# Output projection of a hybrid decoder layer: one weight pool to the end, the group's first sums made a group ahead, norm weights multiplied on GpSimd

## The chip, the cores and the metric

The kernel runs on one core of a Trainium2 chip. The metric is the time of one execution on the device in microseconds (us); lower is better. Before the change three executions took 2694.65, 2693.23 and 2694.86 us, median 2694.65. The engines are named as in the profile: PE (TensorE, with its weight loads PEld), DVE (VectorE), ACT (ScalarE), POOL (GpSimd) and SP (SyncE, which here only issues transfers).

## The reference, cut to what matters

One layer on 256 tokens of width 4096, in float32. The input is normalised and projected by `w_in` (4096 x 21024); two token mixers (a sliding-window attention and a gated delta rule) run on the projections and are merged by gates. What this change touches is the end:

```
merged = sigmoid(gate_a) * y_a + sigmoid(gate_b) * y_b
out = einsum('btd,de->bte', merged, w_o)        # 256 x 4096 by 4096 x 4096
x = x + rms_norm(out, post_norm_g)              # out * rsqrt(mean(out^2) + eps) * post_norm_g
```

## The kernel before, in words

**Precision.** PE multiplies numbers of a rounded 32-bit type. To keep float32 accuracy each weight tile `raw` is split in two: `hi` is the rounded copy, made by ACT (line 174), and `lo` is what the rounding left, made by DVE as `raw - hi` (line 175). A product (`product`, lines 865 to 868) is three matmuls into the same PSUM bank: activations hi by weights hi, hi by lo, lo by hi. `split` works on 1024 columns of a tile at a time, so each call is one ACT cast and one DVE subtraction of 128x1024.

**Order.** The kernel is written in program order and a planner in the framework orders the instructions of each engine when the kernel is compiled: it lets time pass by its own estimates and gives an engine, whenever that is free, the ready instruction that comes first by priority and then by program order. `urgent(2)` marks the splits and the sums of weights as the most pressing, `urgent(1)` the copies out of PSUM; matmuls, transfers and the work of `beside` have none. A tile comes from a pool with a fixed number of buffers, and its first writer waits until the last reader of the buffer's old content is done. On the chip each engine then runs its list strictly in order.

**The stages at the end.** After the merge, `chunk(0)` (line 880) makes the first 512 of the 4096 output columns: 8 loads of 1 MB (`load`, line 190), each split in two units, each unit 12 matmuls. Then pools are closed (lines 994 to 996): `mpool` (the merged activations), `evpool`, and the pool `weights` with 3 buffers each of `raw` (1 MB), `hi` and `lo` (512 KB). A new pool `weights2` takes their place, with 3 buffers of `raw` and 4 each of `hi` and `lo` (`wide`), and the pool `outp` for the output.

Then come three blocks (`block`, line 899), each 1024 output columns in 8 groups of 512 rows of `w_o`. A block computes its 2 x 2 product (two halves of 128 tokens, two halves of 512 columns) with seven products instead of eight for part of the rows, so some products use sums of weight tiles. Per group there are two loads of 1 MB, `rs` (line 913) and `rp` (line 914), and six units, each split and then multiplied: two sums of rs (`tt`, line 918, and line 919, which writes over the second tile of rs) and unit one, rs[0:2]; unit two, rp[0:2]; unit three, rs[2:4]; unit four, rp[2:4]; unit five, the sums tt[0:2]; unit six, the sum tt[2]. Lines 929 and 934 make the other sums. A group is 15 products, 45 matmuls of 512 columns, into eight PSUM banks.

When a block ends, ACT copies its eight banks to SBUF (line 955), and the rest is done while the next block runs: `sums` and `more` on DVE (lines 957 to 966), `norm` on ACT (squares, line 970), and `scale` (lines 972 to 976): for each half a load of the norm's weights `pg` (one buffer, `pg_load`) and one DVE multiplication of 128x1024. The work beside the third block's results falls into `chunk(7)`, which makes the last 512 columns; there the four loads of `x` (`xr`, line 1023) also run. `finish` (line 1028) scales and adds, and stores the output.

Of the kernel before, what the change touches and what calls it, by code (L numbers as in the profile page):

```python
# [8 lines left out]
F32 = mybir.dt.float32  # L9
F32R = mybir.dt.float32r  # L10
# [43 lines left out]
def tile_hybrid_mixer(  # L54
# [18 lines left out]
    V, S, G, PE = nc.vector, nc.scalar, nc.gpsimd, nc.tensor  # L73

    cp = ctx.enter_context(tc.tile_pool(name="consts", bufs=1, side="left"))
    wpool_ = tc.tile_pool(name="weights", bufs=3, side="left")
    wp = wpool_.__enter__()
    evpool = tc.tile_pool(name="evac", bufs=4, side="left")
    ev = evpool.__enter__()
    mp = ctx.enter_context(tc.tile_pool(name="psmain", bufs=5, space=PSUM))  # L80
# [78 lines left out]
        return tc.high_priority(offset=1000000 * level)  # L159

    newest = {}
    wide = {}
    unit = [0]


    def split(raw, extra=False):
        if extra:
            both = wp.tile([P, 4, 512], F32R, name="both", tag="raw")
            hi, lo = both[:, 0:2], both[:, 2:4]
        else:  # L170
            hi = wp.tile([P, 2, 512], F32R, name="hi", **wide)
            lo = wp.tile([P, 2, 512], F32R, name="lo", **wide)
        with urgent(2):
            newest["hi"] = S.copy(hi, raw).ins  # L174
            newest["lo"] = V.tensor_tensor(lo, raw, hi.bitcast(F32), op=ALU.subtract).ins  # L175
        return hi, lo
# [722 lines left out]
    def block(b, beside):  # L899
# [5 lines left out]
        def raws(k2):  # L905
            raw = wp.tile([P, 4, 512], F32, name="raw")
            src = w_o[k2 * 256:k2 * 256 + 256, n0:n0 + 1024].rearrange("(k p) n -> p k n", p=P)
            nc.sync.dma_start(raw.rearrange("p (k h) n -> p k (h n)", k=2), src)
            return raw

        for c in range(8):
            f, l = c == 0, c == 7
            rs = raws(2 * c)
            rp = raws(2 * c + 1)
            kt = 4 * c
            tt = op_.tile([P, 3, 512], F32, name="tt")
            with urgent(2):
                V.tensor_tensor(tt[:, 0], rs[:, 1], rs[:, 3], op=ALU.add)
                V.tensor_tensor(rs[:, 1], rs[:, 0], rs[:, 1], op=ALU.add)
            hi, lo = split(rs[:, 0:2])  # L920
            product(m1, *plain(kt, 0), hi[:, 0], lo[:, 0], f, l)
            product(m5, *form(c, 1), hi[:, 1], lo[:, 1], f, l)
            hi, lo = split(rp[:, 0:2])
            product(m2, *plain(kt + 2, 0), hi[:, 0], lo[:, 0], f, False)
            product(m3, *plain(kt + 2, 0), hi[:, 1], lo[:, 1], f, False)
            product(n4, *plain(kt + 2, 1), hi[:, 0], lo[:, 0], f, False)
            product(x8, *plain(kt + 2, 1), hi[:, 1], lo[:, 1], f, False)
            with urgent(2):
                V.tensor_tensor(tt[:, 1], rs[:, 1], rs[:, 3], op=ALU.add)
            hi, lo = split(rs[:, 2:4])  # L930
            product(m2, *plain(kt + 1, 0), hi[:, 0], lo[:, 0], False, False)
            product(m3, *form(c, 0), hi[:, 1], lo[:, 1], False, False)
            with urgent(2):
                V.tensor_tensor(tt[:, 2], tt[:, 1], rs[:, 2], op=ALU.add)
            hi, lo = split(rp[:, 2:4])
            product(m2, *plain(kt + 3, 0), hi[:, 0], lo[:, 0], False, l)
            product(m3, *plain(kt + 3, 0), hi[:, 1], lo[:, 1], False, l)
            product(x8, *plain(kt + 3, 1), hi[:, 1], lo[:, 1], False, l)
            product(n4, *plain(kt + 3, 1), hi[:, 0], lo[:, 0], False, False)
            hi, lo = split(tt[:, 0:2])  # L940
            product(m7, *form(c, 3), hi[:, 0], lo[:, 0], f, l)
            product(m6, *form(c, 2), hi[:, 1], lo[:, 1], f, l)
            hi = wp.tile([P, 2, 512], F32R, name="hi", **wide)
            lo = wp.tile([P, 2, 512], F32R, name="lo", **wide)
            with urgent(2):
                S.copy(hi[:, 0], tt[:, 2])
                V.tensor_tensor(lo[:, 0], tt[:, 2], hi[:, 0].bitcast(F32), op=ALU.subtract)
            product(n4, *plain(kt + 1, 1), hi[:, 0], lo[:, 0], False, l)
            if c in beside:
                beside[c]()  # L950
        st = op_.tile([P, 4, 512], F32, name="st")
        w1, w2 = slice(n0, n0 + 512), slice(n0 + 512, n0 + 1024)
        with urgent(1):
            for d_, bank in ((st[:, 0], m1), (st[:, 1], m5), (u[:, 0, w1], m2), (u[:, 0, w2], m3), (u[:, 1, w2], x8), (st[:, 3], m7), (st[:, 2], m6), (u[:, 1, w1], n4)):
                S.copy(d_, bank)

        def sums():
# [14 lines left out]
        def scale():  # L972
            for h in range(2):
                pg = pg_load(1 + 2 * b + h)
                cs = slice(n0 + 512 * h, n0 + 512 * h + 512)
                V.tensor_tensor(u[:, :, cs], u[:, :, cs], mid(pg, 2), op=ALU.mult)

        return {0: sums, 1: more, 2: norm, 4: scale}

# [13 lines left out]
    ps, _ = chunk(0, forms)  # L993
    mpool.__exit__(None, None, None)
    evpool.__exit__(None, None, None)
    wpool_.__exit__(None, None, None)
    wp = ctx.enter_context(tc.tile_pool(name="weights2", bufs=3, side="left"))
    wide = {"bufs": 4}
    op_ = ctx.enter_context(tc.tile_pool(name="outp", bufs=1, side="left"))
    u = op_.tile([P, 2, D], F32, name="u")  # L1000
    so = R[:, 0:18].rearrange("p (a b) -> p a b", a=2)
# [87 lines left out]
```

## Time and profile before

| | us |
|---|---|
| median of three executions | 2694.65 |
| the profiled execution | 2694.28 |
| its span in the profile | 2692.6 |
| PE busy in the span | 2666.9 |
| DVE busy | 1769.8 |
| ACT busy | 1330.6 |
| POOL busy | 38.5 |

The span runs from the first to the last instruction that the profile shows; the execution's own time is 1.68 us more. Busy time is summed over the span, and a matmul counts as busy until its modelled end, so matmuls overlap and small gaps of PE don't show in it; the distance from one matmul's start to the next tells more. Line numbers are those of the kernel before.

### The profile page before, as it was taken

The numbers are of one execution on the slowest core, as the hardware profiler recorded it, in microseconds if no ns is written. First come the engines' busy times: TensorE is split into PE (matmuls) and PEld (weight loads), VectorE is DVE, ScalarE is ACT, GpSimd is POOL, SyncE is SP. The second block draws the span as 40 slices with busy tenths as digits, with TensorE's granted clock in tenths as the row PEclk, the third lists the DMA queues.
The fourth block names the chain that finished last, engine by engine and source line by source line (L and its number), as shares of the span: only waits on it lengthen the run. The fifth ranks groups of instructions, "written<-read, shape, count | busy, mean of one in ns | idle before, by whom it ended". The sixth has DMA issues, their size and how long they took to land.

```text
span 2692.6 us, 37957 instructions
## 1 busy us (share of the span) xinstructions
PE 2666.9 (99%) x15164; PEld 2311.8 (86%) x15164; DVE 1769.8 (66%) x2463; ACT 1330.6 (49%) x1926; POOL 38.5 (1%) x59
## 2 busy tenths in 40 slices
PE   9999999999999999999999999999999999989998
PEld 7888888888888888888888888888888888867876
DVE  8785876776776454555554665665555555869996
ACT  7445445545445444444444544555444444546554
POOL 0100100000000000000000000000000000000000
PEclk9999999999999999999999999999999999999999
DMA  8554555655555555565665455455566655645556
GB/s 276 166 178 156 185 173 164 191 165 168 185 174 168 192 188 188 188 189 190 193 193 193 150 180 171 157 180 166 190 192 192 190 188 188 191 175 191 207 213 242
DMA packets 249425, 499.90 MB, mean 186 GB/s; under 512 B 22048, under 2 KB 22688, under 8 KB 248736
## 3 DMA queue, kind: packets, MB, share of 16 engines
q1 hardware_dynamic: 247952, 495.36, 56.6%
q8 instruction: 119, 1.95, 0.3%
q10 hardware_dynamic: 1296, 2.11, 0.2%
q14 instruction: 58, 0.48, 0.0%
HBM read 491.93 MB, written 5.24 MB: 185 GB/s over the span
## 4 chain that ended last, share of the span: by engine, by line
PE 90%; DVE 6%; issue 1%; DMA 1%; ACT 1%; SPq 0%; POOL 0%; DVEq 0%; POOLq 0%; ACTq 0%
PE mm L232 48%; PE mm L233 25%; DVE lo L175 3%; PE mm L867 3%; PE mm L868 3%; PE mm L866 2%; PE mm L226 2%; PE sd L868 1%; PE sd L867 1%; PE sd L866 1%; PE mm L225 1%; DVE pr L508 1%; DVE xs L509 1%; DMA xt<-in_xT_dram 1%; PE sd L769 1%
## 5 line engine op out<-in xcount | busy, mean ns | idle before, releaser
L232 PE MATMUL mm<-hT,hi 128*128 128x512 f32 x5083 | 1788.4, 393 | 0.2 <-ACT hi L185 0.2
L175 DVE TENSOR_TENSOR lo<-raw,hi 128x1024 fp32r<-128x1024 f32 x909 | 1106.1, 1223 | 745.2 <-ACT hi L174 743.4
L174 ACT CAST hi<-raw 128x1024 fp32r<-128x1024 f32 x909 | 948.4, 1049 | 1183.8 <-PE mm L232 1042.9
L233 PE MATMUL mm<-hT,lo 128*128 128x256 f32 x5083 | 1435.2, 282 | 2.2 <-DVE lo L175 1.4
L232 PEld LDWEIGHTS mm<-hT,hi 128*128 128x128 f32 x5083 | 954.2, 188 | 199.8 <-issue 7.9
L233 PEld LDWEIGHTS mm<-hT,lo 128*128 128x128 f32 x5083 | 960.3, 189 | 16.6 <-DVE lo L175 8.4
L232 PE MATMUL mm<-gbs,hi 128*128 128x512 f32 x480 | 168.0, 390 | 0.0
L232 PE MATMUL mm<-gas,hi 128*128 128x512 f32 x480 | 168.0, 390 | 0.0
L233 PE MATMUL mm<-gbs,lo 128*128 128x256 f32 x480 | 135.3, 282 | 0.0
L233 PE MATMUL mm<-gas,lo 128*128 128x256 f32 x480 | 135.3, 282 | 0.0
L866 PE MATMUL mm<-hi,ms 128*128 128x512 f32 x268 | 106.6, 400 | 8.2 <-ACT hi L174 8.2
L867 PE MATMUL mm<-lo,ms 128*128 128x512 f32 x268 | 107.0, 399 | 0.3 <-DVE lo L175 0.3
L868 PE MATMUL mm<-hi,ms 128*128 128x512 f32 x268 | 106.5, 397 | 0.0
L232 PEld LDWEIGHTS mm<-gas,hi 128*128 128x128 f32 x480 | 90.1, 188 | 17.8
L232 PEld LDWEIGHTS mm<-gbs,hi 128*128 128x128 f32 x480 | 90.1, 188 | 17.8
L241 ACT COPY cr<-mm 128x256 f32<-128x256 f32 x228 | 83.8, 367 | 20.1 <-PE mm L226 18.1
L233 PEld LDWEIGHTS mm<-gbs,lo 128*128 128x128 f32 x480 | 90.7, 189 | 1.3
L233 PEld LDWEIGHTS mm<-gas,lo 128*128 128x128 f32 x480 | 90.6, 189 | 1.3
L866 PEld LDWEIGHTS mm<-hi,ms 128*128 128x128 f32 x268 | 50.4, 189 | 22.5 <-ACT hi L174 10.7
L226 PE MATMUL mm<-hT,hi 128*128 128x512 f32 x164 | 64.3, 392 | 0.0
L867 PEld LDWEIGHTS mm<-lo,ms 128*128 128x128 f32 x268 | 50.7, 189 | 14.7 <-DVE lo L175 2.4
L868 PEld LDWEIGHTS mm<-hi,ms 128*128 128x128 f32 x268 | 50.7, 189 | 11.8
(313 smaller groups left out, 2001.3 us busy)
## 6 DMA issues: line engine op xcount, KB each, us to landing
raw<-in_w_in_dram SPq DMA_DIRECT2D x326, 1024.0 KB, 5.1
raw<-in_w_o_dram SPq DMA_DIRECT2D x64, 1024.0 KB, 6.3
raw<-in_w_pb_dram SPq DMA_DIRECT2D x32, 1024.0 KB, 5.5
raw<-in_w_pa_dram SPq DMA_DIRECT2D x32, 1024.0 KB, 5.5
xr<-in_x_dram SPq DMA_DIRECT2D x4, 1024.0 KB, 8.8
xt<-in_xT_dram SPq DMA_DIRECT2D x7, 512.0 KB, 9.4
blx<-d SPq DMA_DIRECT2D x16, 128.0 KB, 5.5
pg<-in_post_norm_g_dram SPq DMA_DIRECT2D x8, 256.0 KB, 4.9
```

The costliest lines, as they stand in the source:

```text
L174: newest["hi"] = S.copy(hi, raw).ins
L175: newest["lo"] = V.tensor_tensor(lo, raw, hi.bitcast(F32), op=ALU.subtract).ins
L225: PE.matmul(ps[nt][:, T:512], lo[:, kk, c], m[:, 0:T], start=False, stop=False, skip_group_check=True)
L226: PE.matmul(ps[nt], hi[:, kk, c], m, start=False, stop=True, skip_group_check=True)
L232: PE.matmul(ps[nt], hi[:, kk, c], m, start=(kt == 0), stop=False, skip_group_check=True)
L233: newest["product"] = PE.matmul(ps[nt][:, T:512], lo[:, kk, c], m[:, 0:T], start=False, stop=False, skip_group_check=True).ins
L241: S.copy(cr, ps[:, T:512])
L508: V.tensor_tensor(pr[:, :, 0:i + 1], xs3[:, :, 0:i + 1], mid(bl3[:, i, 0:i + 1], 8), op=ALU.mult)
L509: V.tensor_reduce(xs3[:, :, i], pr[:, :, 0:i + 1], axis=AX.X, op=ALU.add, negate=True)
L866: PE.matmul(bank, xh, wh, start=start, stop=False, skip_group_check=True)
L867: PE.matmul(bank, xh, wl, start=False, stop=False, skip_group_check=True)
L868: PE.matmul(bank, xl, wh, start=False, stop=stop, skip_group_check=True)
```

## The change

The pool `weights` stays open to the end of the kernel and is used by the blocks and the last chunk too; `weights2` and `wide` are gone. It has 3 buffers each of raw, hi and lo. In the blocks every fourth hi tile comes from the output pool instead (`hi4`, one buffer), so that hi has 4 buffers in all and lo has 3.

The sums of a group change. Called with a group's number, `first_sums` loads rs and makes two sums at once in one DVE instruction of 128x1024 (t57). It is called for group 0 ahead of the loop and for group c+1 inside group c, between the third and the fourth unit in program order. The first unit of a group is now the split of t57, with the products into m5 and m7. The other two sums (t64) are made one after the other, each 128x512. The raw tile rs[0] is split alone (`split1`) as the group's last unit, so rs is held from its load until the last unit of its own group, and rp until the fourth. The eight banks are copied out in another order. In `scale` the multiplication by the norm's weights is issued to POOL (`G`) in place of DVE (`V`).

```diff
@@ -73,8 +73,7 @@
     V, S, G, PE = nc.vector, nc.scalar, nc.gpsimd, nc.tensor
 
     cp = ctx.enter_context(tc.tile_pool(name="consts", bufs=1, side="left"))
-    wpool_ = tc.tile_pool(name="weights", bufs=3, side="left")
-    wp = wpool_.__enter__()
+    wp = ctx.enter_context(tc.tile_pool(name="weights", bufs=3, side="left"))
     evpool = tc.tile_pool(name="evac", bufs=4, side="left")
     ev = evpool.__enter__()
     mp = ctx.enter_context(tc.tile_pool(name="psmain", bufs=5, space=PSUM))
@@ -159,17 +158,24 @@
         return tc.high_priority(offset=1000000 * level)
 
     newest = {}
-    wide = {}
+    turn = [0]
+
+    def hi_tile(fourth=None):
+
+        turn[0] += fourth is not None
+        if fourth is not None and turn[0] % 4 == 0:
+            return fourth.tile([P, 2, 512], F32R, name="hi4")
+        return wp.tile([P, 2, 512], F32R, name="hi")
     unit = [0]
 
 
-    def split(raw, extra=False):
+    def split(raw, extra=False, fourth=None):
         if extra:
             both = wp.tile([P, 4, 512], F32R, name="both", tag="raw")
             hi, lo = both[:, 0:2], both[:, 2:4]
         else:
-            hi = wp.tile([P, 2, 512], F32R, name="hi", **wide)
-            lo = wp.tile([P, 2, 512], F32R, name="lo", **wide)
+            hi = hi_tile(fourth)
+            lo = wp.tile([P, 2, 512], F32R, name="lo")
         with urgent(2):
             newest["hi"] = S.copy(hi, raw).ins
             newest["lo"] = V.tensor_tensor(lo, raw, hi.bitcast(F32), op=ALU.subtract).ins
@@ -908,50 +914,64 @@
             nc.sync.dma_start(raw.rearrange("p (k h) n -> p k (h n)", k=2), src)
             return raw
 
+        def first_sums(c):
+
+            rs = raws(2 * c)
+            t57 = op_.tile([P, 2, 512], F32, name="t57")
+            with urgent(2):
+                V.tensor_tensor(t57, rs[:, 0:4:3], mid(rs[:, 1], 2), op=ALU.add)
+            return rs, t57
+
+        def split1(raw):
+            hi = hi_tile(op_)
+            lo = wp.tile([P, 2, 512], F32R, name="lo")
+            with urgent(2):
+                S.copy(hi[:, 0], raw)
+                V.tensor_tensor(lo[:, 0], raw, hi[:, 0].bitcast(F32), op=ALU.subtract)
+            return hi, lo
+
+        rs, t57 = first_sums(0)
         for c in range(8):
             f, l = c == 0, c == 7
-            rs = raws(2 * c)
             rp = raws(2 * c + 1)
             kt = 4 * c
-            tt = op_.tile([P, 3, 512], F32, name="tt")
+            t64 = op_.tile([P, 2, 512], F32, name="t64")
+            hi, lo = split(t57, fourth=op_)
+            product(m5, *form(c, 1), hi[:, 0], lo[:, 0], f, l)
+            product(m7, *form(c, 3), hi[:, 1], lo[:, 1], f, l)
             with urgent(2):
-                V.tensor_tensor(tt[:, 0], rs[:, 1], rs[:, 3], op=ALU.add)
-                V.tensor_tensor(rs[:, 1], rs[:, 0], rs[:, 1], op=ALU.add)
-            hi, lo = split(rs[:, 0:2])
-            product(m1, *plain(kt, 0), hi[:, 0], lo[:, 0], f, l)
-            product(m5, *form(c, 1), hi[:, 1], lo[:, 1], f, l)
-            hi, lo = split(rp[:, 0:2])
+                V.tensor_tensor(t64[:, 0], t57[:, 0], rs[:, 3], op=ALU.add)
+            hi, lo = split(rp[:, 0:2], fourth=op_)
             product(m2, *plain(kt + 2, 0), hi[:, 0], lo[:, 0], f, False)
             product(m3, *plain(kt + 2, 0), hi[:, 1], lo[:, 1], f, False)
             product(n4, *plain(kt + 2, 1), hi[:, 0], lo[:, 0], f, False)
             product(x8, *plain(kt + 2, 1), hi[:, 1], lo[:, 1], f, False)
             with urgent(2):
-                V.tensor_tensor(tt[:, 1], rs[:, 1], rs[:, 3], op=ALU.add)
-            hi, lo = split(rs[:, 2:4])
+                V.tensor_tensor(t64[:, 1], t64[:, 0], rs[:, 2], op=ALU.add)
+            hi, lo = split(rs[:, 2:4], fourth=op_)
             product(m2, *plain(kt + 1, 0), hi[:, 0], lo[:, 0], False, False)
             product(m3, *form(c, 0), hi[:, 1], lo[:, 1], False, False)
-            with urgent(2):
-                V.tensor_tensor(tt[:, 2], tt[:, 1], rs[:, 2], op=ALU.add)
-            hi, lo = split(rp[:, 2:4])
+            ra = rs[:, 0]
+            if not l:
+                nxt = first_sums(c + 1)
+            hi, lo = split(rp[:, 2:4], fourth=op_)
             product(m2, *plain(kt + 3, 0), hi[:, 0], lo[:, 0], False, l)
             product(m3, *plain(kt + 3, 0), hi[:, 1], lo[:, 1], False, l)
             product(x8, *plain(kt + 3, 1), hi[:, 1], lo[:, 1], False, l)
             product(n4, *plain(kt + 3, 1), hi[:, 0], lo[:, 0], False, False)
-            hi, lo = split(tt[:, 0:2])
-            product(m7, *form(c, 3), hi[:, 0], lo[:, 0], f, l)
-            product(m6, *form(c, 2), hi[:, 1], lo[:, 1], f, l)
-            hi = wp.tile([P, 2, 512], F32R, name="hi", **wide)
-            lo = wp.tile([P, 2, 512], F32R, name="lo", **wide)
-            with urgent(2):
-                S.copy(hi[:, 0], tt[:, 2])
-                V.tensor_tensor(lo[:, 0], tt[:, 2], hi[:, 0].bitcast(F32), op=ALU.subtract)
-            product(n4, *plain(kt + 1, 1), hi[:, 0], lo[:, 0], False, l)
+            hi, lo = split(t64, fourth=op_)
+            product(n4, *plain(kt + 1, 1), hi[:, 1], lo[:, 1], False, l)
+            product(m6, *form(c, 2), hi[:, 0], lo[:, 0], f, l)
+            hi, lo = split1(ra)
+            product(m1, *plain(kt, 0), hi[:, 0], lo[:, 0], f, l)
+            if not l:
+                rs, t57 = nxt
             if c in beside:
                 beside[c]()
         st = op_.tile([P, 4, 512], F32, name="st")
         w1, w2 = slice(n0, n0 + 512), slice(n0 + 512, n0 + 1024)
         with urgent(1):
-            for d_, bank in ((st[:, 0], m1), (st[:, 1], m5), (u[:, 0, w1], m2), (u[:, 0, w2], m3), (u[:, 1, w2], x8), (st[:, 3], m7), (st[:, 2], m6), (u[:, 1, w1], n4)):
+            for d_, bank in ((st[:, 1], m5), (st[:, 3], m7), (u[:, 0, w1], m2), (u[:, 0, w2], m3), (u[:, 1, w2], x8), (u[:, 1, w1], n4), (st[:, 2], m6), (st[:, 0], m1)):
                 S.copy(d_, bank)
 
         def sums():
@@ -973,7 +993,7 @@
             for h in range(2):
                 pg = pg_load(1 + 2 * b + h)
                 cs = slice(n0 + 512 * h, n0 + 512 * h + 512)
-                V.tensor_tensor(u[:, :, cs], u[:, :, cs], mid(pg, 2), op=ALU.mult)
+                G.tensor_tensor(u[:, :, cs], u[:, :, cs], mid(pg, 2), op=ALU.mult)
 
         return {0: sums, 1: more, 2: norm, 4: scale}
 
@@ -993,9 +1013,6 @@
     ps, _ = chunk(0, forms)
     mpool.__exit__(None, None, None)
     evpool.__exit__(None, None, None)
-    wpool_.__exit__(None, None, None)
-    wp = ctx.enter_context(tc.tile_pool(name="weights2", bufs=3, side="left"))
-    wide = {"bufs": 4}
     op_ = ctx.enter_context(tc.tile_pool(name="outp", bufs=1, side="left"))
     u = op_.tile([P, 2, D], F32, name="u")
     so = R[:, 0:18].rearrange("p (a b) -> p a b", a=2)
```

## Rows read from the trace of the kernel before

**Rows 1.** The page's first part: busy time of each engine, its share of the span, instructions.

```profile
PE 2666.9 (99%) x15164; PEld 2311.8 (86%) x15164; DVE 1769.8 (66%) x2463; ACT 1330.6 (49%) x1926; POOL 38.5 (1%) x59
```

**Rows 2.** Busy time by stretch (from:to in us, length, then busy us and instructions of PE, PEld, DVE, ACT, POOL, then the granted clock of PE as a share of full speed, the share of the DMA engines and GB/s): the end of chunk 0, the change of pools, and block 0 behind it.

```profile
2360.00:2372.00 12.00, 12.00 (x53) 9.50 (x51) 3.06 (x3) 2.50 (x3) 0.00 (x0) 1.00 0.00 0
2372.00:2386.00 14.00, 5.95 (x15) 4.11 (x15) 9.83 (x11) 5.98 (x9) 0.00 (x0) 0.63 0.73 262
2386.00:2457.00 71.00, 71.00 (x306) 57.16 (x305) 61.38 (x68) 38.58 (x41) 0.00 (x0) 1.00 0.56 204
```

**Rows 3.** Timeline at the change of pools (start, duration, engine, line, operation; in brackets the engine's idle time before and what ended it).

```profile
2371.82 0.40 PE L868 MATMUL mm<-hi,ms 128*128 128x512 f32 x1
2372.24 1.39 SPq L908 DMA_DIRECT2D raw<-in_w_o_dram  x3
2377.43 0.69 DVE L918 TENSOR_TENSOR tt<-raw 128x512 f32<-128x512 f32 x1 [3.69 <-DMA raw<-in_w_o_dram]
2378.88 3.95 ACT L174 CAST hi<-raw 128x1024 fp32r<-128x1024 f32 x4 [5.87 <-DVE raw L919]
2379.98 0.80 PE L866 MATMUL mm<-hi,ms 128*128 128x512 f32 x1 [7.77 <-ACT hi L174]
...
2382.51 0.63 PE L867 MATMUL mm<-lo,fx 128*128 128x512 f32 x1
```

**Rows 4.** DVE's timeline over the last loads of chunk 0: the splits of its units eleven, thirteen and fifteen (counted from 0), the last readers of its last three raw buffers.

```profile
2353.79 1.22 DVE L175 TENSOR_TENSOR lo<-raw,hi 128x1024 fp32r<-128x1024 f32 x1 [0.79 <-ACT hi L174]
...
2359.39 1.23 DVE L175 TENSOR_TENSOR lo<-raw,hi 128x1024 fp32r<-128x1024 f32 x1 [1.59 <-ACT hi L174]
...
2364.93 1.23 DVE L175 TENSOR_TENSOR lo<-raw,hi 128x1024 fp32r<-128x1024 f32 x1 [1.57 <-ACT hi L174]
...
2372.33 0.69 DVE L986 TENSOR_TENSOR u<-mm,pg 128x512 f32<-128x512 f32 x1 [6.17 <-ACT st L982]
```

**Rows 5.** PE's timeline: the first matmul of group 2 of block 0, of block 1, of block 2 and of chunk 7.

```profile
2403.82 0.40 PE L866 MATMUL mm<-hi,ms 128*128 128x512 f32 x1
...
2466.81 0.40 PE L866 MATMUL mm<-hi,ms 128*128 128x512 f32 x1
...
2551.73 0.40 PE L866 MATMUL mm<-hi,ms 128*128 128x512 f32 x1
...
2636.64 0.40 PE L866 MATMUL mm<-hi,ms 128*128 128x512 f32 x1
```

**Rows 6.** DVE's timeline in group 2 of block 1, where it finishes the results of block 0 between the splits.

```profile
2487.41 1.22 DVE L976 TENSOR_TENSOR u<-u,pg 128x1024 f32<-128x1024 f32 x1
2488.54 4.63 DVE L175 TENSOR_TENSOR lo<-raw,hi 128x1024 fp32r<-128x1024 f32 x4
```

**Rows 7.** DVE's timeline in one group of block 0 (lines 929 and 934 stand between the first two rows, with the same 0.69).

```profile
2399.09 0.69 DVE L918 TENSOR_TENSOR tt<-raw 128x512 f32<-128x512 f32 x1
...
2401.89 2.39 DVE L175 TENSOR_TENSOR lo<-raw,hi 128x1024 fp32r<-128x1024 f32 x2
2404.45 2.36 DVE L175 TENSOR_TENSOR lo<-raw,hi 128x1024 fp32r<-128x1024 f32 x2 [0.18 <-ACT hi L174]
2406.73 1.22 DVE L175 TENSOR_TENSOR lo<-tt,hi 128x1024 fp32r<-128x1024 f32 x1
2408.87 0.69 DVE L947 TENSOR_TENSOR lo<-tt,hi 128x512 fp32r<-128x512 f32 x1 [0.92 <-ACT hi L946]
```

**Rows 8.** Waits of the queue that issues transfers, 2385 to 2640 us: who waited, for whom, us in total, times, longest.

```profile
SPq L908 <- DVE lo L175: 174.3, 42, 9.9
```

**Rows 9.** Line 908, from issue to landing, for a load issued at 2405.71 with none before it under way, and for one issued at 2417.34, 1.13 us behind another.

```profile
DMA to landing us min/median/max: 5.1/5.1/5.1
...
DMA to landing us min/median/max: 7.2/7.2/7.2
```

**Rows 10.** ACT's timeline, a group's first cast in block 0.

```profile
2400.68 1.05 ACT L174 CAST hi<-raw 128x1024 fp32r<-128x1024 f32 x1 [2.34 <-DVE raw L919]
```

**Rows 11.** POOL's groups of instructions by form over the whole span: line, operation, shapes, count, busy us and mean ns, idle before.

```profile
L467 POOL TENSOR_SCALAR_AFFINE_SELECT dec<-dec 128x512 f32<-128x512 f32 x8 | 8.3, 1039 | 143.3 <-ACT dec L466 143.3
L656 POOL TENSOR_TENSOR f<-o,mhalf 128x8 f32<-128x8 f32 x4 | 7.4, 1844 | 552.5 <-DVE o L655 552.5
```

**Rows 12.** Timelines of POOL and DVE around three of the selects of line 467: one with DVE idle, one that starts while DVE is in a subtraction, and one during which DVE starts a multiplication of two tiles.

```profile
482.75 0.64 POOL L467 TENSOR_SCALAR_AFFINE_SELECT dec<-dec 128x512 f32<-128x512 f32 x1 [40.59 <-ACT dec L466]
...
99.03 1.23 DVE L175 TENSOR_TENSOR lo<-raw,hi 128x1024 fp32r<-128x1024 f32 x1 [1.54 <-ACT hi L174]
...
99.57 1.18 POOL L467 TENSOR_SCALAR_AFFINE_SELECT dec<-dec 128x512 f32<-128x512 f32 x1 [4.35 <-ACT dec L466]
...
283.29 0.64 POOL L467 TENSOR_SCALAR_AFFINE_SELECT dec<-dec 128x512 f32<-128x512 f32 x1 [5.61 <-ACT dec L466]
...
283.63 0.83 DVE L460 TENSOR_TENSOR gm<-triu,glo 128x512 fp32r<-128x512 f32 x1
```

**Rows 13.** The queue that issues transfers (start, time to issue, line, what is loaded, how many): pg's first load at the end of chunk 0, and then chunk 7.

```profile
2353.09 0.34 SPq L990 DMA_DIRECT2D pg<-in_post_norm_g_dram  x1
...
2649.67 0.34 SPq L990 DMA_DIRECT2D pg<-in_post_norm_g_dram  x1
...
2650.58 0.93 SPq L195 DMA_DIRECT2D raw<-in_w_o_dram  x2
...
2664.65 0.37 SPq L195 DMA_DIRECT2D raw<-in_w_o_dram  x1
```

## The prediction

> **What bounds the kernel now.** I read the page first: PE is busy for 99% of the span, DVE for 66%, ACT for 49% [rows 1]. So time can only come from PE's few gaps or from fewer matmuls, and the change keeps every matmul. I then read the stages. In the last microseconds of chunk 0 PE has no gap and DVE is mostly idle; in the 14 us from 2372 on PE is busy for 5.95 us at a mean granted clock of 0.63; behind that it is full again [rows 2]. The timeline says why: the last matmul of chunk 0 starts at 2371.82, only then (2372.24) are the first three raw loads of block 0 issued, the first sum starts at 2377.43, the cast at 2378.88, and PE's next matmul at 2379.98 [rows 3].
>
> How long is a block without stalls? From group 2 of block 0 to block 1 are six groups in 2466.81 - 2403.82 = 62.99 us [rows 5]: 10.50 us a group of 45 matmuls, 0.2333 a matmul, 84.0 a block. Chunk 0 ends at 2371.82 + 0.23 = 2372.05. Block 1 starts at 2466.81, so block 0 took 94.76 from there, 10.76 too long: 7.93 are the pause, the rest is the wait for the first `lo` and the matmuls at half speed, 1.2 of 2.4 GHz, each 0.63 us long in place of 0.40 [rows 3]. Blocks 1 and 2 took 84.92 and 84.91 [rows 5], 0.92 too long each: there DVE puts the results of the block before between the splits and starts four splits in a row late [rows 6]. All that this part of the kernel loses is 10.76 + 1.83 = 12.6 us, 0.47% of the time. More the change cannot give.
>
> **The change of pools.** With one pool the loads of block 0 need only a free raw buffer. Those come free with the splits at 2353.79 + 1.22 = 2355.0, 2359.39 + 1.23 = 2360.6 and 2364.93 + 1.23 = 2366.2 [rows 4]. A lone load lands after 5.1 us [rows 9], so rs, rp and the next rs land by 2360.2, 2365.8 and 2371.4. t57 then has an idle DVE (1.2 us), its split 1.05 [rows 10] and 1.22 when chunk 0 frees a hi and a lo, each unit being 2.8 us (12 x 0.2333) of PE: all is done before 2372.05. What can be late next is the first bank, if m5 gets one that chunk 0 held until DVE read it (two times 0.69 from 2372.33 [rows 4]): 0 to 1.7 us. I take 0, since three of five banks are free. This part removes 10.8 us, and the slow clock with it.
>
> **The loop through the raw buffers.** This is what the change adds, and the trace of before shows it only in pieces. There loads are issued the moment a split frees a buffer (174.3 us of waiting on `lo` [rows 8]) and still land early enough: PE is full. Now rs is held from its early sum to the last unit of its group, so rp of the next group must take the buffer that unit four frees. That closes a loop: issue 0.04, landing 5.1 [rows 9], cast of unit two 1.05 [rows 10] and 0.06 for two signals, subtraction of unit two 1.13, of unit three 1.13, of unit four 1.22 (two in a row take 2.36 [rows 7]). Sum 9.73 us, 0.77 under PE's 10.50. But in program order the next `first_sums` stands ahead of unit four, at a priority that lets it go first once its rs has landed: 1.13 more (as 128x1024 in rows 7), 10.86, so PE waits 0.36 in each turn. If t64's second sum sits in it too (0.61 to 0.73, the distance of such sums), it is 11.5 and 1.0 a turn. A block has seven turns, so 21 in all: 0, 7.6 or 21 us. Which it is hangs on the next rs, issued 1.2 to 1.9 us behind rp and landing some 3.2 behind it (7.2 + 1.13 - 5.1 [rows 9]); rp's cast and two subtractions take 3.4. That is a tie, and I take a third of 7.6: 2.5 us.
>
> **Sums and buffers.** Four sums of 128x512 become one of 128x1024 and two of 128x512, the same elements in one instruction less; per group DVE was busy for 10.50 - 0.18 - 0.92 = 9.40 us [rows 7] and saves at most 0.16. ACT no longer waits for line 919 (2.34 us a group [rows 10]), which cost PE nothing. hi keeps four buffers, lo loses one: unit n's subtraction waits until PE is done with unit n-3. Chunk 0 runs with three of each and no gap [rows 2], but its units are equal; here the shortest lead is what PE needs for units five and six, 9 matmuls or 2.1 us, less 1.2 for the subtraction: 0.9 us. Steady groups pay nothing for that, disturbed ones do. The new order of copies out of PSUM follows the new order of use: 0.
>
> **The multiplication on POOL.** DVE loses six instructions of 1.22 us [rows 6], two per block. On POOL none of this kind is in the trace. A select of half the size with one input takes 0.64 us [rows 12]; twice the elements is 1.3, which is the lower bound. The only two-tensor instructions there are powers, 1.84 us for 8 elements a partition [rows 11], which by element would be 236 us: the far end, beyond reason for a product. Twice the elements and twice the inputs of the select is 2.5 us, and I take that, as the select is nearest in size.
>
> It does not run beside DVE for free. A select that started 0.54 us into a subtraction took 1.18 us in place of 0.64, and a DVE product that started during a select took 0.83 in place of 0.69 [rows 12]: each waits for the other. So each of the four multiplications in blocks 1 and 2 can hold DVE for 2.5 us against a lead of 0.9 to 3; the 1.13 that DVE no longer spends comes back. That replaces the 1.83 us by 0 to 10, and I take 1.2 a block, 2.4.
>
> The Trainium skill (SBUF — State Buffer, "SBUF: two separate sides") says that DVE and GpSimd share a port pair which one of them holds for its whole instruction, a DVE instruction with two SBUF inputs included. The trace agrees (1.18 against 0.64). By that rule every one of these DVE instructions excludes POOL's, and the move gives DVE's time back and more. The skill's GPSIMD Engine Reference, section 3.1, has 4497 ns for 2048 elements, an estimate of 2.25 us here, 0.25 below my value; no run here shows it.
>
> **Chunk 7.** pg's second load waits for the first multiplication, and two raw loads stand behind it on SP's queue (2649.67, 2650.58 [rows 13]). Ending 1.3 us later there, or 2.5 with the wait for DVE, shifts those loads and the last one (2664.65), which has no slack: 0 to 2.5 us, if the planner keeps that order; I take 0.8. The two multiplications and the loads of pg between and behind them fit into the 44.8 us (192 matmuls) of chunk 7.
>
> **Sum.** The profiled execution is 2694.28: the span 2692.6 and 1.68 around it; the median is 0.37 more, within the spread. 2694.28 - 10.76 - 1.83 + 2.5 + 2.4 + 0.8 = 2687.4. Two times of this kernel differ for certain beyond 0.2%, 5.4 us: my gain of 6.9 is just above.
>
> **Rivals.**
> 1. The loop binds in each turn with the next group's first sum in it: 7.6 in place of 2.5, so 2692.5, no change. For: program order puts it there, and the tie above. Against: while rp is on its way DVE has time for other ready work, t57 included. Chance 0.18.
> 2. The lock is paid in full, four times 2.5, in place of 2.4: 2695.0, no change. This is the page's rule with nothing absorbed. For: the rows on both sides. Against: DVE has 1.1 us of idle time in a group of before, and a load of pg keeps the two multiplications of a block apart. Chance 0.12.
> 3. Slower: the loop of 11.5 us. A planner that expects loads to land sooner than they do puts both sums ahead of unit four, and each turn then costs 1.0: 2687.4 - 2.5 + 21 = 2705.9. Nothing is gained from a loop of 10.95 on, 0.45 a turn ((6.9 + 2.5) / 21), and it is slower for certain from 0.70 a turn. For: nothing in the raw buffers is spare now. Against: a load alone lands in 5.1 us each time. Chance 0.12.
> 4. The change doesn't do what it says: block 0's loads still wait, since the output pool must wait for the closed ones. Then 2694.28 + 3.9 or so, 2698. Against: pg lies in that pool too, and its first load was issued at 2353.09 [rows 13], 19 us before chunk 0 ended. Chance 0.03.
>
> My forecast, 2683 to 2690, has 0.55. The range is 2682.5 to 2698: it goes from almost no loss to both "no change" cases. Faster 0.55, same 0.31, slower 0.14.
>
> **What would show it.** PE's matmuls 0.23 apart across the end of chunk 0 and a granted clock of 1.00 there show the first step. Block lengths tell the loop: 84.0 is free, 86.5 rival 1, 91 rival 3, with PE waiting on unit two's cast and ACT on a raw load. POOL's multiplication near 2.5 us, and a DVE subtraction of over 1.3 beside it, show the lock. I am wrong if block 0, which has no POOL work, is over 87 us, or if PE still stops for 8 us before it.

## The result and the profile after

The changed kernel takes 2708.07 us (median of 4; 2706.07 to 2709.13) against 2694.45 before: the ratio is 1.005, 95% interval 1.0033 to 1.0068. The forecast was 2687.4, faster; it is slower. The profiled execution took 2707.23, its span is 2705.5.

The page's first part, after [rows 1]:

```profile
PE 2676.6 (99%) x15164; PEld 2310.2 (85%) x15164; DVE 1765.5 (65%) x2433; ACT 1328.9 (49%) x1926; POOL 53.7 (2%) x65
```

The engines do what was expected: POOL has 15 us more, DVE 4 less. The matmuls are the same; PE's longer busy time is matmuls that wait or run at half speed. Busy time by stretch [rows 2] (columns as there), and two stretches of 3.4 us in blocks 1 and 2:

```profile
2360.00:2372.00 12.00, 12.00 (x53) 9.67 (x52) 8.10 (x9) 5.69 (x7) 0.00 (x0) 1.00 0.54 177
2372.00:2386.00 14.00, 14.00 (x62) 11.27 (x61) 12.54 (x14) 8.38 (x12) 0.00 (x0) 1.00 0.47 169
2386.00:2457.00 71.00, 69.58 (x288) 52.87 (x287) 55.76 (x57) 35.74 (x41) 0.00 (x0) 1.00 0.52 185
...
2486.90:2490.30 3.40, 3.40 (x9) 2.65 (x8) 3.40 (x3) 0.59 (x1) 1.93 (x1) 0.51 0.12 41
2596.10:2599.50 3.40, 3.40 (x9) 2.66 (x10) 3.40 (x4) 0.47 (x1) 0.00 (x0) 0.51 0.00 0
```

The first two rows show the gain: where PE was busy for 5.95 of 14 us at a clock of 0.63, it is now full at 1.00. The third shows the loss beginning: block 0, which has no POOL work, is no longer full. In the last two the clock is at its lower level, 1.2 of 2.4 GHz. PE's timeline, the first matmul of blocks 0, 1, 2 and of chunk 7 [rows 5]:

```profile
2371.91 0.40 PE L872 MATMUL mm<-hi,fx 128*128 128x512 f32 x1
...
2460.18 0.40 PE L872 MATMUL mm<-hi,fx 128*128 128x512 f32 x1
...
2552.56 0.40 PE L872 MATMUL mm<-hi,fx 128*128 128x512 f32 x1
...
2649.42 0.40 PE L872 MATMUL mm<-hi,ms 128*128 128x512 f32 x1
```

Block 0 starts where chunk 0 ends, but the blocks take 88.27, 92.38 and 96.86 us in place of 84.0: 25.5 us lost, against 12.6 before. Block 0, which has no POOL work, is over the 87 us that the prediction named as a sign of being wrong.

One turn of the raw buffers in block 0: the queue that issues transfers, then ACT, then DVE (t is t57 on line 922, t64's second sum on line 950), then the queue again, and PE at unit two.

```profile
2399.02 0.37 SPq L914 DMA_DIRECT2D raw<-in_w_o_dram  x1
2400.76 0.37 SPq L914 DMA_DIRECT2D raw<-in_w_o_dram  x1
...
2404.20 2.94 ACT L180 CAST hi<-raw 128x1024 fp32r<-128x1024 f32 x3 [3.20 <-DMA raw<-in_w_o_dram]
...
2401.37 0.69 DVE L950 TENSOR_TENSOR t<-t,raw 128x512 f32<-128x512 f32 x1
...
2405.28 2.36 DVE L181 TENSOR_TENSOR lo<-raw,hi 128x1024 fp32r<-128x1024 f32 x2 [1.51 <-ACT hi L180]
2407.73 1.23 DVE L922 TENSOR_TENSOR t<-raw 128x1024 f32<-128x1024 f32 x1
2408.87 1.22 DVE L181 TENSOR_TENSOR lo<-raw,hi 128x1024 fp32r<-128x1024 f32 x1
...
2410.12 0.37 SPq L914 DMA_DIRECT2D raw<-in_w_o_dram  x1
...
2406.56 0.50 PE L873 MATMUL mm<-lo,ms 128*128 128x512 f32 x1 [0.15 <-DVE lo L181]
```

rp is issued at 2399.02, unit two's cast waits for it until 2404.20, DVE subtracts units two and three, makes t57, subtracts unit four, and at 2410.12 the next rp takes the buffer: 11.10 us, where PE's group is 10.50. PE pays at unit two: its first matmul with the new `lo` waits for DVE (2406.56). There is a second loop in the same rows: the next rs, issued at 2400.76, lands 6.9 us later (2407.7), just as DVE gets to t57; behind t57 come units four, five and the last, and then the next rs. It is 11.1 us long too.

Block 2, with POOL's multiplications (line 996): POOL, DVE, the transfer queue, PE.

```profile
2577.09 2.38 POOL L996 TENSOR_TENSOR u<-u,pg 128x1024 f32<-128x1024 f32 x1 [86.29 <-ACT st L990]
2583.03 3.20 POOL L996 TENSOR_TENSOR u<-u,pg 128x1024 f32<-128x1024 f32 x1 [3.56 <-DMA pg<-in_post_norm_g_dram]
...
2577.98 3.71 DVE L181 TENSOR_TENSOR lo<-raw,hi 128x1024 fp32r<-128x1024 f32 x2 [1.46 <-ACT hi L180]
...
2582.75 1.21 DVE L181 TENSOR_TENSOR lo<-raw,hi 128x1024 fp32r<-128x1024 f32 x1
2583.88 3.43 DVE L181 TENSOR_TENSOR lo<-t,hi 128x1024 fp32r<-128x1024 f32 x1
...
2579.50 7.10 SPq L1010 DMA_DIRECT2D pg<-in_post_norm_g_dram  x2
2586.70 13.03 SPq L914 DMA_DIRECT2D raw<-in_w_o_dram  x3
...
2594.72 0.73 PE L872 MATMUL mm<-hi,ms 128*128 128x512 f32 x2 [2.85 <-ACT hi L180]
```

A multiplication that starts with DVE idle takes 2.38 us; one that starts during a DVE subtraction takes 3.20. Subtractions that start during a multiplication are held too: a pair takes 3.71 us in place of 2.36, and one takes 3.43 in place of 1.22. The subtraction that frees rp's buffer ends at 2583.96, but the raw load is issued only at 2586.70: on the queue ahead of it stands the second load of pg, which waits until POOL is done with the old pg (2586.23). POOL uses what it brings only at 2659.09, in chunk 7. PE stops for 2.85 us, and the half clock follows.

### The profile page after: what moved, and what is told of

Read it like the earlier page. It is cut to its first block, busy times and chain, and to the rows that moved or that the text cites. A ratio compares the mean times of both kernels' runs of the same rounds, so it can differ in the third digit from the quotient of the medians.

```text
span 2705.5 us, 38007 instructions
## 1 busy us (share of the span) xinstructions
PE 2676.6 (99%) x15164; PEld 2310.2 (85%) x15164; DVE 1765.5 (65%) x2433; ACT 1328.9 (49%) x1926; POOL 53.7 (2%) x65
## 5 line engine op out<-in xcount | busy, mean ns | idle before, releaser
L181 DVE TENSOR_TENSOR lo<-raw,hi 128x1024 fp32r<-128x1024 f32 x885 | 1086.6, 1232 | 779.6 <-ACT hi L180 773.4
L180 ACT CAST hi<-raw 128x1024 fp32r<-128x1024 f32 x885 | 922.6, 1049 | 1190.1 <-PE mm L238 1041.0
L872 PEld LDWEIGHTS mm<-hi,ms 128*128 128x128 f32 x268 | 49.3, 189 | 23.7 <-ACT hi L180 13.1
L181 DVE TENSOR_TENSOR lo<-t,hi 128x1024 fp32r<-128x1024 f32 x48 | 60.8, 1267 | 6.0 <-PE sd L873 4.4
```

The source lines that it names most:

```text
L872: PE.matmul(bank, xh, wh, start=start, stop=False, skip_group_check=True)
```

## The experiments

The questions: how much of the 25.5 us is the loop through the raw buffers, how much POOL's multiplications, do the two add up, and is the first step worth its 10.8? Block lengths are taken as above, for blocks 0, 1 and 2. A fourth raw buffer would test the loop most directly; it was not tried.

**First: the multiplications back on DVE.**

```diff
-                G.tensor_tensor(u[:, :, cs], u[:, :, cs], mid(pg, 2), op=ALU.mult)
+                V.tensor_tensor(u[:, :, cs], u[:, :, cs], mid(pg, 2), op=ALU.mult)
```

> The changed kernel with the six norm multiplications back on DVE, all else kept. Changed kernel: 2708.1, its blocks 88.3, 92.4 and 96.9 us against 84.0 without a stall. Theory S (two costs that add up: the loop through the raw buffers 4.3 a block, POOL's multiplications the 4.1 and 8.6 that blocks 1 and 2 lose on top): the 12.7 go, and the six multiplications of 1.22 us lengthen single turns on DVE by 0 to 1.2 each, four of them in blocks: 2695.4 to 2700.3, block 0 unchanged at 88.3. Theory P (POOL is nearly all, and disturbs what comes behind it for whole groups): 2690 or less, block 0 below 87. Theory L (the loop is nearly all, and a multiplication in it costs the same on either engine): 2704 to 2708, blocks 1 and 2 still at 92 or more. The multiplications should show as DVE rows of 1.2 us and no subtraction over 1.3.

Measured: 2697.64 us, ratio to before 1.0012 (1.0003 to 1.0021); blocks 87.51, 89.22, 90.64. 10.4 us come back, as theory S has it, and block 0 keeps its loss: the loop is there without POOL.

**Second: first sums behind unit four, POOL kept.**

```diff
-            if not l:
-                nxt = first_sums(c + 1)
             hi, lo = split(rp[:, 2:4], fourth=op_)
...
             product(n4, *plain(kt + 3, 1), hi[:, 0], lo[:, 0], False, False)
+            if not l:
+                nxt = first_sums(c + 1)
```

> The changed kernel with the next group's first sums issued behind unit four instead of ahead of it, so that t57 is no longer in the way of the load that unit four's subtraction releases; POOL keeps the multiplications. Theory S: the loop's 9.73 lies under PE's 10.50, block 0 falls from 88.3 to 84.0 to 84.5, the three blocks give back 12.8, and POOL's 12.7 stay: about 2695.3. Theory L: with 0.77 us of slack a turn the late loads of blocks 1 and 2 are absorbed too, 2683 to 2687. Theory P: 2704 or more.

Measured: 2685.15, ratio 0.9966 (0.9953 to 0.9978); blocks 84.00, 85.74, 85.75. 22.9 us come back by moving one call over one unit: theory L's time. Block 0 is free of loss. The two costs don't add up, so theory S falls: with slack in the loop most of POOL's is absorbed too. POOL and DVE in block 1 of this run:

```profile
2492.26 2.45 POOL L996 TENSOR_TENSOR u<-u,pg 128x1024 f32<-128x1024 f32 x1 [3.15 <-DMA pg<-in_post_norm_g_dram]
...
2487.00 5.46 DVE L181 TENSOR_TENSOR lo<-raw,hi 128x1024 fp32r<-128x1024 f32 x3 [0.16 <-PE mm L873]
2492.38 3.42 DVE L922 TENSOR_TENSOR t<-raw 128x1024 f32<-128x1024 f32 x1
```

POOL holds DVE as before (three subtractions 5.46 in place of 3.6, t57 3.42 in place of 1.22), but no load waits for t57 any more.

**Third: both edits.**

> Both edits: first sums behind unit four and the multiplications on DVE. Theory S: 2682.6 to 2685, each block 84.0 to 85. Theory P and theory L give the same within 3 us, so this run tells whether anything else costs time: over 2687 says that a third cost (three lo buffers in place of four, or the new order of units) is there.

Measured: 2681.75 (2681.37 to 2683.36), ratio 0.9953 (0.9939 to 0.9966); blocks 84.00, 83.99, 83.99. In the blocks nothing else costs time, and this version beats both kernels: 12.6 us under the kernel before, 26.3 under the changed one. DVE in one group of block 0:

```profile
2403.15 3.62 DVE L181 TENSOR_TENSOR lo<-raw,hi 128x1024 fp32r<-128x1024 f32 x3 [0.16 <-PE mm L873]
2406.70 1.22 DVE L922 TENSOR_TENSOR t<-raw 128x1024 f32<-128x1024 f32 x1
...
2412.26 1.23 DVE L181 TENSOR_TENSOR lo<-t,hi 128x1024 fp32r<-128x1024 f32 x1 [1.06 <-PE sd L873]
2413.65 3.63 DVE L181 TENSOR_TENSOR lo<-raw,hi 128x1024 fp32r<-128x1024 f32 x3 [0.16 <-PE mm L873]
```

Units two to four in one go, 10.50 from group to group, and DVE now waits for PE, no longer PE for DVE. Against this run the place of t57 costs 2697.64 - 2681.75 = 15.9 us with the multiplications on DVE, and POOL costs 3.4 us with slack in the loop, 10.4 without.

**Fourth: the kernel before with the pool kept open, three buffers each.**

```diff
-    wpool_ = tc.tile_pool(name="weights", bufs=3, side="left")
-    wp = wpool_.__enter__()
+    wp = ctx.enter_context(tc.tile_pool(name="weights", bufs=3, side="left"))
...
-    wpool_.__exit__(None, None, None)
-    wp = ctx.enter_context(tc.tile_pool(name="weights2", bufs=3, side="left"))
-    wide = {"bufs": 4}
```

> The kernel before with one edit: the weight pool stays open, with 3 buffers each of raw, hi and lo to the end (no fourth hi and lo). The stop at the change of pools goes: 2694.45 - 10.8 = 2683.7 if the fourth buffers are worth nothing. If they are worth something, the blocks come out longer than 84.9: at 86 it is 2687, at 88.4 nothing is gained. The rival, that the old order of units would keep the loads of block 0 waiting even so, gives 2690 or more.

Measured: 2692.36, ratio 0.9992 (0.9984 to 1.0001). A miss at first sight: the stop is gone (PE 13.98 of the 14 us from 2372 on, at 1.00), but 8.7 us are lost later, in many small stops behind ACT's casts. One of them on PE:

```profile
2470.25 0.50 PE L865 MATMUL mm<-hi,ms 128*128 128x512 f32 x1 [0.33 <-ACT hi L173]
```

**Fifth: two buffers for pg in the changed kernel.**

```diff
-        pg = op_.tile([P, 512], F32, name="pg")
+        pg = op_.tile([P, 512], F32, name="pg", bufs=2)
```

> The changed kernel with two buffers for the norm weights (pg) instead of one, so that no load of pg waits on SP's queue for a multiplication on POOL, with raw loads behind it. Of the 10.4 us by which the first experiment was faster than the changed kernel, the two that held POOL's lock alone cost 3.4 (second against third experiment). Theory Q (the queue): the other 7 are the raw load of block 2 issued at 2586.70 where the subtraction that freed its buffer ended at 2583.97, the like in block 1, and the half clock behind PE's stop: 2701 to 2704. Theory K (the lock alone, multiplied because a loop without slack passes each delay of a subtraction on to a load): 2707 to 2708.5, nothing gained.

Measured: 2704.35, 1.0034 (1.0022 to 1.0046); blocks 89.49, 92.24, 93.71. 3.7 us come back, all in block 2 (96.86 before), just short of theory Q. So the queue is about half of the 7. In block 1 nothing comes back, and the expectation was wrong there. DVE and the transfer queue in block 1 of the changed kernel:

```profile
2488.49 3.39 DVE L181 TENSOR_TENSOR lo<-raw,hi 128x1024 fp32r<-128x1024 f32 x1
...
2485.24 5.92 SPq L1010 DMA_DIRECT2D pg<-in_post_norm_g_dram  x2
2491.91 2.12 SPq L914 DMA_DIRECT2D raw<-in_w_o_dram  x2
```

The pg loads are out of the way at 2491.16; the raw load waits for the subtraction, which POOL holds until 2491.88. The rest of the 7 fits DVE held like this in a loop without slack, but no run separates it. Block 0, which this edit doesn't touch, is 1.2 longer here: the loop's cost moves that far between two runs with the same code there.

**Sixth and seventh: the fourth experiment with four hi and four lo, and with four hi and three lo.** Sixth (in the seventh lo always comes from `wp`):

```diff
+        four = blk and turn[0] % 4 == 0
+        hi = (op_.tile([P, 2, 512], F32R, name="hi4") if four else wp.tile([P, 2, 512], F32R, name="hi"))
+        lo = (op_.tile([P, 2, 512], F32R, name="lo4") if four else wp.tile([P, 2, 512], F32R, name="lo"))
```

> The kernel before with the weight pool open throughout and, in the blocks, every fourth hi and every fourth lo from the output pool, so that both have four buffers as before. The fourth experiment with three of each gave 2692.4 where 2683.7 was expected. If the missing fourth buffers are the whole difference: 2683.7, blocks of 84.9. If the old order of units loses something else that the long stop hid: 2687 or more.

> The same with four hi buffers and three lo, the numbers of the changed kernel, in the old order of units. ACT's wait for a hi was the last one ahead of PE's stops in the fourth experiment (PE idle behind ACT's cast), so hi is the one that counts: within 1.5 us of the run with four of both, 2683.7 to 2685. The rival, that lo counts as much: half of the difference to 2692.4 or more stays, 2688 or more.

Measured: 2684.03 (ratio 0.996, 0.9948 to 0.9973) and 2685.43 (0.9967, 0.9955 to 0.998). The sixth is as expected; the seventh is 0.4 above its range, but within 1.5 us of the sixth as forecast. The open pool is worth 10.3 us by itself, the fourth hi 6.9 of the 8.3 that three buffers lose, the fourth lo 1.4. In the new order of units the third experiment has no loss with three lo.

**Eighth: the kernel before with only the multiplications on POOL** (the first diff, the other way).

> The kernel before with the six multiplications on POOL and nothing else. Theory K and the lock with slack: as in the second experiment 0.87 per multiplication in the blocks, 3.4, less the 1.83 that the blocks of before lose behind DVE's own multiplication: 2694.45 + 1.6 = 2696. If the lock is paid in full: 4 x 2.5 - 1.83, 2702.6. If DVE's saved time is worth more than the lock: under 2693.

Measured: 2705.21, 1.0045 (1.0032 to 1.0058): 10.8 us slower, more than the lock paid in full. Theory K and the lock with slack fell for the old order. DVE and the transfer queue in block 1:

```profile
2488.00 8.51 DVE L175 TENSOR_TENSOR lo<-raw,hi 128x1024 fp32r<-128x1024 f32 x4 [0.42 <-ACT hi L174]
...
2489.85 5.94 SPq L990 DMA_DIRECT2D pg<-in_post_norm_g_dram  x2
2495.89 12.01 SPq L908 DMA_DIRECT2D raw<-in_w_o_dram  x4
```

The four splits in a row of [rows 6] take 8.51 instead of 4.63, and the raw loads stand behind pg until 2495.89. Busy time by stretch (columns as in [rows 2]) shows the granted clock behind PE's first stop:

```profile
2491.00:2495.00 4.00, 4.00 (x11) 3.14 (x12) 4.00 (x3) 1.04 (x1) 2.00 (x1) 0.57 0.16 59
```

How the 10.8 us divide among the lock, the queue and the clock was not measured for this order.

**Ninth and tenth: the same DVE work added inside and outside the loop.** The third experiment, with the subtraction of unit two done twice, or that of unit five:

```diff
-            hi, lo = split(rp[:, 0:2], fourth=op_)
+            hi, lo = split(rp[:, 0:2], fourth=op_, times=2)
```

> The third experiment (2681.75, no loss in the loop) with the subtraction of unit two done twice in every group: 1.13 us more of DVE inside the loop of the raw buffers (load, cast of unit two, subtractions of units two, three and four, next load), while the next group's first sum stays behind it. The loop's own length then is 0.04 + 5.14 + 1.05 + 0.06 + 3.62 + 1.13 + 0.03 = 11.07 against PE's 10.50. Theory LL (the length of the loop is what the changed kernel lost): 0.57 in each of 21 turns, block 0 at 88.0, 2693.7 in all. Theory W (the loss came from t57 itself, which waited for a late load with unit four's subtraction behind it): nothing of that kind here, block 0 below 85, under 2686.

> The control: the same 1.13 us of DVE added in every group, but outside the loop, by doing the subtraction of the fifth unit (t64's) twice. DVE then has about 10.4 us of work in a group of 10.50. Theory LL: block 0 stays at 84.0 to 85; blocks 1 and 2, where DVE also has the results of the block before, 5.7 us of sums and 2.4 of multiplications, lose up to 6 each because DVE itself is full; 2682 to 2694. If any added DVE work of this size costs the same wherever it stands (theory D: DVE is the bound): block 0 at 88 like the run above.

Measured: 2706.73 (1.0043, 1.0027 to 1.006) with block 0 at 90.94, and 2688.58 (0.998, 0.997 to 0.9989) with block 0 at 84.09. DVE as the bound (theory D) falls: the same 1.13 us a group is free in block 0 outside the loop. (Of the 6.8 us that the tenth loses to the third, 4.1 are in chunk 7, 48.9 us in place of 44.8, where no subtraction is doubled; why stays open.) Inside, three of block 0's eight groups are 11.05 long, as worked out, but others reach 12.5, and the total is 13 over the forecast. The doubled subtraction also hands unit two to PE later, which frees hi and lo later, so this run doesn't show the loop of the loads alone. Hence the last two.

**Eleventh and twelfth: each raw load in two halves**, t57 held where it was on DVE; multiplications on DVE, then on POOL.

```diff
-            nc.sync.dma_start(raw.rearrange("p (k h) n -> p k (h n)", k=2), src)
+            for k in range(2):
+                nc.sync.dma_start(raw[:, 2 * k:2 * k + 2].rearrange("p h n -> p (h n)"), src[:, k])
...
+            with tc.issue_after(newest["t57"]):
+                hi, lo = split(rp[:, 2:4], fourth=op_)
```

> The first experiment (changed kernel, multiplications on DVE, 2697.6) with each raw load of the blocks issued as two loads of half the size, so that unit two's cast, which needs only the first half of rp, starts earlier; t57 is held between the subtractions of units three and four in every group, as it was, so the order on DVE stays and only the landing in the loop is shorter. Before, issue to landing took 5.14 us of a loop of 11.1. Theory LL (the loop of load, cast and subtractions is what binds): if the first half lands in 3.2 to 4.4, the loop is 9.2 to 10.4, under PE's 10.50: block 0 falls from 87.5 to 84.0 to 85, the run to 2683 to 2687. Theory W (t57 waits for its late rs and holds up unit four): rs lands no sooner as a whole, so nothing is gained, 2696 or more. Theory D (the place of t57 on DVE costs PE directly): the same, 2696 or more.

> The same loads in halves with the multiplications on POOL, that is the changed kernel with only the loads halved and t57 pinned where it was. Theory LL with slack: the loop no longer binds, and POOL costs what it cost in the second experiment, 3.4 on top of the run beside it: 2686.5 to 2691. If POOL's cost does not depend on the loop: 10.4 on top, 2693 or more.

Measured: 2694.71 (1.0001, 0.9992 to 1.001), blocks 85.11, 87.30, 90.31; and 2698.55 (1.0016, 1.0007 to 1.0026), blocks 86.57, 90.32, 90.64. A miss in between: 2.9 us come back instead of 11 to 15. Block 0 alone is nearly as theory LL has it (84.0 to 85), blocks 1 and 2 are not. The transfer queue, ACT and DVE in block 0 of the eleventh:

```profile
2398.43 0.81 SPq L915 DMA_DIRECT2D raw<-in_w_o_dram  x2
...
2402.01 2.95 ACT L180 CAST hi<-raw 128x1024 fp32r<-128x1024 f32 x3 [2.46 <-DMA raw<-in_w_o_dram]
...
2403.09 2.36 DVE L181 TENSOR_TENSOR lo<-raw,hi 128x1024 fp32r<-128x1024 f32 x2 [0.49 <-ACT hi L180]
2407.10 1.22 DVE L923 TENSOR_TENSOR t<-raw 128x1024 f32<-128x1024 f32 x1 [1.65 <-DMA raw<-in_w_o_dram]
2408.24 1.22 DVE L181 TENSOR_TENSOR lo<-raw,hi 128x1024 fp32r<-128x1024 f32 x1
...
2414.16 2.36 DVE L181 TENSOR_TENSOR lo<-raw,hi 128x1024 fp32r<-128x1024 f32 x2 [0.50 <-ACT hi L180]
2418.31 1.23 DVE L923 TENSOR_TENSOR t<-raw 128x1024 f32<-128x1024 f32 x1 [1.79 <-DMA raw<-in_w_o_dram]
```

The first half of rp lands sooner (the cast starts 3.6 us after the issue, in place of 5.2), so rp's loop is cut by 1.6. But now DVE stands idle for 1.65 us in front of t57, for the second half of rs, with unit four ready behind it. From turn to turn t57 comes 10.5 to 11.3 us apart in block 0 (11.21 in these rows), 11.0 in the mean of five turns; two of PE's groups there take 11.07 and 10.97, the others 10.50 to 10.56. I read this as theories LL and W both right in part: two loops of nearly one length run through t57, and shortening one leaves the other. It is a reading of these rows; no run shortens the loop of rs alone, and theory D, the place of t57 costing PE directly, forecast the same total as W. What is shown without that is that moving t57 behind unit four (third against first experiment) removes the whole loss. POOL adds 3.8 us here, near the 3.4 beside slack.

## Why the prediction was wrong

**The change of pools: right.** The three loads of block 0 were issued at 2354.90, 2360.50 and 2366.20, each within 0.1 of the times worked out; block 0 follows chunk 0 without a gap, and no bank was late. Worth 10.8 by the sum, 10.3 by the sixth experiment, the kernel before with the pool open and four hi and four lo as it had.

**The block changes: right.** The third experiment's blocks are 84.0; 2694.28 - 10.76 - 1.83 = 2681.7, measured 2681.75.

**The loop through the raw buffers: the step that failed.** "That is a tie, and I take a third of 7.6: 2.5 us." It costs 15.9 us with the multiplications on DVE. The chain and its members were right: issue, landing 5.1, casts and subtractions, 10.86 worked out, 11.10 measured (units two and three end 0.2 later than I added up). Two things were wrong. The prediction spoke of t57 as going first "once its rs has landed", as if DVE chose at run time, though the section on the kernel before says that each engine runs its list in order. The list was fixed beforehand: t57 stands ahead of unit four in every turn shown, and where rs is late (1.65 us in the eleventh experiment, where the order was prescribed) unit four waits behind it. (The Trainium skill, Perfetto Trace Analysis, "Tensor Engine Instruction (MATMUL, LD_WEIGHTS)", calls the queues of ACT, DVE and GPSIMD strictly first in, first out; these rows agree.) So a tie is no chance of paying a third: the excess is paid in full, and what DVE waits for rs in front of t57 (0 to 0.25 us a turn in block 0 of the first experiment) comes on top. And the loop of rs itself (landing 6.9, t57, units four, five and the last) was not worked out; it is as long as the other. In the first experiment block 0 lost 3.5 us, 0.50 a turn in place of rival 1's 0.36; blocks 1 and 2 lost 5.2 and 6.6. There DVE also has the sums and multiplications of the block before, which may lengthen turns; no run takes them out. Rival 1 had the mechanism and half the price, and 0.18.

**The multiplication on POOL: price right, effect missed.** 2.5 was taken for one, 2.38 to 2.41 is measured where DVE was idle at its start, and each engine waits for the other as forecast. But 1.2 a block was taken, 2.4 in all, and 10.4 is measured. That is the size of rival 2, "paid in full", but by luck: 3.7 of it came back with a second buffer for pg, so it is not the lock alone. What the prediction left out stands in the rows of block 2 above: the raw load behind pg's on the transfer queue (which it saw for chunk 7 and not for the blocks) and the half clock behind the stop. With slack in the loop the same six instructions cost 3.4.

The Trainium skill (SBUF — State Buffer, "SBUF: two separate sides") says that an instruction of DVE with two SBUF inputs and one of GpSimd that reads SBUF keep each other out for their whole length. This trace agrees: 3.43 us in place of 1.22. An estimate from the figure in the Trainium skill's GPSIMD Engine Reference, section 3.1, was 2.25 us for one multiplication; 2.38 is measured.

**Fewer lo buffers, copies out, chunk 7: right, or nearly.** They cost 0, 0 and 0: the third experiment's blocks show no loss, and chunk 7, for which 0.8 was taken, took 44.8 in the changed kernel. Only in the old order of units do the fourth buffers show a price (sixth and seventh experiment).

**The sum in hindsight:** 2694.28 - 10.76 - 1.83 + 15.9 + 10.4 = 2708.0, measured 2708.07. The last two terms are differences of runs that lead from the third experiment to the changed kernel, so they close by construction; what the sum tests is the gain, 2681.7 against the third experiment's 2681.75. The slower rival's number, 2705.9, came near, but not by its mechanism: t64's second sum is not in the loop (it ends at 2402.06 in the rows of block 0, ahead of unit two's cast). Its "for", that nothing in the raw buffers is spare now, was the heart of the matter.

## What to carry to other kernels

Where a change holds a buffer longer, write down every loop that runs through it (load, cast, each instruction in the queue ahead of the release, next load), compare each with PE's period, and count an instruction that is queued ahead of the release in full: t57 kept its place ahead of unit four even where its load was late. The same POOL work cost 3.4 us beside a loop with some 0.5 us of slack (10.50 less the 9.94 of the ninth experiment's sum without its added 1.13) and 10.4 beside one without. The place of one call cost 15.9 us, more than the 12.6 that the rest of the change gains without POOL. And look at what stands on the transfer queue ahead of an urgent load: a load that isn't needed yet, and whose buffer is still in use, holds it up.

## What was not expected of the hardware

A stop of PE of 2.85 us was followed by 3.4 us at the half clock, which is 1.7 us of PE's work; the stop of 1.41 that ended at 2486.35 was as well, while that of 1.43 us in the fifth experiment's block 1 was followed by none; why they differ stays open. The half clock didn't always cost time: the group around the stop of 1.41 took 14.64 us in the changed kernel, and 14.62 at full clock in the fifth experiment. A load cut in two brings its first half after 3.5 us in place of 5.1, but the rs behind it is complete no sooner. And a block's cost in a loop without slack is not steady: with no POOL work and the same code in each pair, block 0 lost 4.3 us in the changed kernel and 5.5 in the fifth experiment, 1.1 in the eleventh and 2.6 in the twelfth.
